# A hybrid mLSTM / RWKV-7 layer on one core: triangular joins, finished pairs and chunk operands move to other banks, buffers and places in the order

## The chip, the core and the metric

The kernel runs on one core of a Trainium2 chip. A core has five engines that execute their instructions each in its own order: PE (TensorE, matmuls), DVE (VectorE), ACT (ScalarE), POOL (GpSimd) and SP (SyncE, which here only starts DMA transfers). They wait for each other by semaphores. SBUF holds the working data, PSUM the results of matmuls, in eight banks. The metric is the device time of one execution in microseconds: the kernel before takes 3405.07 us, the median of three runs (3402.93 to 3407.92).

## The reference

One layer over 512 latent tokens (x) and 256 context tokens (ctx) of width 2048, in float32. Both go through one input projection, whose output feeds two groups of heads: an mLSTM with four heads and an RWKV-7 with sixteen heads of width 64, each in both directions. The RWKV state is a 64 x 64 matrix per head and direction:

```
def step(s, xs):
    r_t, w_t, k_t, v_t, kk_t, a_t = xs
    s = (s * w_t[:, :, None, :]
         - jnp.einsum("bhvk,bhk->bhv", s, kk_t)[..., None] * (kk_t * a_t)[:, :, None, :]
         + v_t[..., :, None] * k_t[..., None, :])
    return s, jnp.einsum("bhvk,bhk->bhv", s, r_t)
...
y_f, s_f = rwkv7_scan(..., state[2], False)
y_b, s_b = rwkv7_scan(..., state[3], True)
y = y_f + y_b
...
hc = modulate(rms_norm(ctx, g_norm1[layer]), csh1, csc1)
yc, ctx_state = hybrid_mixers(hc, p, zero_state(ctx.shape[0]))
hx = modulate(rms_norm(x, g_norm1[layer]), sh1, sc1)
yx, _ = hybrid_mixers(hx, p, ctx_state)
x = x + gt1 * (yx @ w_out[layer])
hx = modulate(rms_norm(x, g_norm2[layer]), sh2, sc2)
x = x + gt2 * conv_ffn(hx, rows, GRID_W, p)
...
return rms_norm(x, g_final)
```

The scans over x start from the states that the context leaves. The summed y of a head is normalised, gets a bonus term and a gate, and enters the output projection beside the mLSTM heads.

## The kernel before

**Stages.** First the adaLN vectors and the context's projections; then the projections of x, beside which the RWKV heads are worked; then the mLSTM heads and the output projection; then the FFN (from about 1900 us to the end). Float32 products are made of three matmuls with split operands (high and low parts: `whi`, `wlo`, `H`), so a weight tile that a DMA brings is split by ACT (L299) and DVE (L300).

**The RWKV part.** Two heads make a pair (eight pairs), a pair and a direction make a unit. Tokens are cut into chunks of 64 (eight for x, four for ctx). A pair goes through five steps:
- *Preparation*: `pair_shared` (L661) and `prep` (L681) make the decayed keys and, with matmuls into banks "pre" (L747), the 64 x 64 products within a chunk. All that a chunk needs is stored in DRAM (`Sx_d`, `Sc_d`).
- *Solve*: `tsolve` loads the two 32 x 32 diagonal triangles of every 64 x 64 block of two pairs (four context units of pairs), inverts them in thirty row steps on DVE (L798, L799) and stores them.
- *Join*: the off-diagonal block follows from the two inverses by 32 x 32 matmuls (L816, then L821, 64 each for a pair of x), in two R banks. It loads a pair's block into `t_Y`, which has one buffer, transposes it on DVE (L810), copies the first product on ACT (L818) and the second on DVE (L823), and stores the result.
- *Chain*: `chain` steps through the chunks of two pairs at once, four units in a step, both R banks in each step (`chain_step`: matmuls L856 and L859, copies on ACT L870 and L878, state update on DVE L890, outputs L900 and L902). The operands of two chunks come with one load, `chain_load`, into `r_GK` (six buffers of two chunks, L830).
- *Finalization*: `finalize_pair` loads y, normalises it on DVE and ACT, transposes it by four matmuls (L977) in a bank "pre" and multiplies in the gate (L978). `mid()` in a chain runs it a step further: before the yield, then behind it.

**What sets the order.** A queue holds jobs: `solve_q` after preparation, `chain_q` after the solve. Before the preparation of pair p, `x_job(p)` calls a solve (p even) or a chain (p odd) of the two pairs that are ready. Behind the loop over pairs stand `do_solve(2)` (pairs 6 and 7) and, with the mLSTM projections, `do_chain(2)`. The scheduler of the language (it simulates a timeline of its own) then fixes the order of each engine, so what is written earlier has precedence but need not come first. All weight, chunk and adaLN loads are started by SP, one after the other. PSUM has two banks "acc" (projections), four "pre" and two "R". The adaLN accumulation of the later chunks (`ada_late`, rows L232 on DVE: `adacc<-am`) is spread among these jobs. The first half of the output projection (L1268 to L1270) needs mLSTM heads 0 and 1 and pairs 0 to 3, the second half the rest.

Of the kernel before, what the change touches and what calls it, by code (L numbers as in the profile page):

```python
# [15 lines left out]
P = 128  # L16
# [80 lines left out]
def body(tc, A, dbg=None):  # L97
# [679 lines left out]
    def tsolve(pairs):  # L777

        nc_ = 2 * pairs[0][0].nch
        n = 4 * nc_ * len(pairs)  # L780
        x = rp("t_X", [P, 32, 32], 1)[0:n]

        def blocks():
            q = 0
            for us in pairs:
                for r in range(0, P, 32):
                    o = us[0].kc + r % 64
                    yield x[q:q + nc_], us[0].S_d[r:r + 32, :, o:o + 32].rearrange("s c t -> c s t")
                    q += nc_

        for t, g in blocks():
            sp.dma_start(t, g)
        T1 = rp("t_T", [P, 256], 1)[0:n]
        dve.memset(x.rearrange("p s t -> p (s t)")[:, 0:1024:33], 1.0)
        for t in range(30, 0, -1):
            m = 31 - t
            w = T1[:, 0:t * m].rearrange("p (s t) -> p s t", t=m)
            dve.tensor_tensor(w, x[:, 0:t, t:t + 1].to_broadcast([n, t, m]), x[:, t:t + 1, t + 1:32].to_broadcast([n, t, m]), ALU.mult)  # L798
            dve.tensor_tensor(x[:, 0:t, t + 1:32], x[:, 0:t, t + 1:32], w, ALU.add)  # L799
        for t, g in blocks():  # L800
            sp.dma_start(g, t)

        XT = rp("t_X", [P, 2, 16, 32], 1)
        for k, us in enumerate(pairs):
            kc = us[0].kc
            T_d = us[0].S_d[:, :, kc:kc + 64]
            T = rp("t_Y", [P, 16, 64], 1)[:, 0:nc_]
            sp.dma_start(T, T_d)
            W = XT[:, k, 0:nc_]
            dve.transpose(W, T[:, :, 0:32])  # L810
            ws = [PS("R", [P, 16, 32])[:, 0:nc_] for _ in range(2)]
            a_, b_ = ([slice(64 * h + o, 64 * h + o + 32) for h in range(2)] for o in (0, 32))
# [12 lines left out]

    def chain_load(u, tt):

        cu = u.c0 + 2 * tt
        o = rk("r_GK", [P, 2, 512], 6)[:, :, 0:3 * u.kc + 128]
        sp.dma_start(o, u.S_d[:, cu:cu + 2, :])  # L830
        return o

    def chain_v(p, seg, nch):
# [70 lines left out]
    def chain(pairs, mid):  # L904

        x = pairs[0][0].seg == "x"
        nch = pairs[0][0].nch
        Vs, ys = [], []
        for us in pairs:
            Vs.append(chain_v(us[0].p, us[0].seg, nch))  # L910
            ys.append(rk("r_yt", [P, 8, 64], 2) if x else None)
            for u in us:
                if not x:
                    Mst[(u.p, u.d)] = rk("r_M", [P, 64], 16)
                    pool.memset(Mst[(u.p, u.d)], 0.0)
                u.M = Mst[(u.p, u.d)]
        n = nch // 2
        for i in range(n):
            if x and i == 1:
                mid()  # L920
            ops = [[chain_load(u, i if u.d == 0 else n - 1 - i) for u in us] for us in pairs]
            for c in range(2 * i, 2 * i + 2):
                units = []
                for k, (us, os_, V, y) in enumerate(zip(pairs, ops, Vs, ys)):
                    us[0].y = y
                    for j, (u, o) in enumerate(zip(us, os_)):
                        cu = nch - 1 - c if j else c
                        units.append((u, o[:, cu % 2], cu, V, 2 * k + (j if 2 * c < nch - 1 else 1 - j)))
                chain_step(units, c < nch // 2, x and c == nch - 1)
        if x:  # L930
            for us, y in zip(pairs, ys):
                y_d = us[0].y_d = DT("yr_d", [4, P, 128], 8)
                for h in range(2):
                    sp.dma_start(y_d[:, :, 64 * h:64 * h + 64].rearrange("a (b t) v -> t (a b) v", t=64), y[LOHI[1 - h]])
            mid()

    def bonus(p, uf, ub, s):
        kd = uf.kd
# [11 lines left out]
    def finalize_pair(p, uf, ub, bo):  # L950
# [21 lines left out]
        gs = sq.rearrange("p a b -> p (a b)")  # L972
        sp.dma_start(gs, g_d[p])
        yield
        pt = PS("pre", [P, 512])
        for tt in range(4):
            pe.transpose(pt[:, 128 * tt:128 * tt + 128], y[:, tt, :], ident)  # L977
        dve.scalar_tensor_tensor(gs, pt, V("gnb", p), gs, ALU.add, ALU.mult)  # L978
# [37 lines left out]
    def ctx_part(H, k0, k1, part):  # L1016
        for n, (tag, (kind, *ts)) in enumerate(ctx_plan):
            if k0 == 0:
                if tag == "r_y":
                    d = rk("r_y", [P, 512], 2)  # L1020
                else:
                    if n % 2 == 0:
                        pair = am() if tag == "am" else rk("r_GK", [P, 2, 512], 6)
                    d = pair[:, n % 2]
                part.append(d)
            d = part[n][:, 0:512 if kind == "tm" else NC_ * len(ts)]
            pt = PS("acc", [P, 512])[:, 0:d.shape[-1]]
# [86 lines left out]
    Hx = HT(NX)  # L1114
    modulated(xload2, rx, gsc[:, :, 0], mod[:, 0:16], Hx, range(8))

    solve_q, chain_q = [], []

    fin_q = []

# [15 lines left out]
        while fin_q or fin[0] is not None:  # L1136
            fin_step()

    def do_chain(n=1):
        if len(chain_q) >= n:  # L1140
            job = [t for _ in range(n) for t in chain_q.pop(0)]
            chain([us for _, us, _ in job], fin_step)
            fin_q.extend(t for t in job if t[2] is not None)

    def do_solve(n=1):
        if len(solve_q) >= n:
            jobs = [solve_q.pop(0) for _ in range(n)]
            tsolve([us for job in jobs for _, us, _ in job])
            chain_q.extend(jobs)

    def ctx_job(p):
        do_chain()
        job = []
        for pp in range(p, p + 2):
            s = pair_shared(pp, "c")
            job.append((pp, prep(pp, s, "c", DT("Sc_d", [P, 8, 320], 8)), None))
        do_solve()
        solve_q.append(job)

    def x_job(p):  # L1160
        if p < 2:
            do_chain()
        elif p % 2 == 0:
            do_solve(2)
        else:
            do_chain(2)
        s = pair_shared(p, "x")
        S_d = DT("Sx_d", [P, 16, 512], 8)
        us = prep(p, s, "x", S_d, 0) + prep(p, s, "x", S_d, 1)
        job = [(p, us, bonus(p, us[0], us[1], s))]  # L1170
        if p == 0:
            do_solve()
        solve_q.append(job)


    for i, _ in enumerate(ctx_finish(Hc, part)):
# [51 lines left out]
    for p in range(NPAIR):  # L1228
# [12 lines left out]
        for h in range(MH):  # L1241
            if HEAD_AT[h] == p and p < 7:
                x_head(h)
    do_solve(2)
    for h in range(MH):
        if h == CHAIN_H:
            do_chain(2)
        if HEAD_AT[h] == 7:
            x_head(h)
        for _ in range(LATE_H[h]):  # L1250
# [37 lines left out]
    assert not chain_q and not solve_q  # L1288
    ahead_[0] = AHEAD
    Hm.more(2)  # L1290
    for k in KORD[8:]:
# [215 lines left out]
```

## Time and profile before

| | |
|---|---|
| median of three runs | 3405.07 us |
| profiled execution, and its span | 3401.15 us, 3399.3 us |
| busy in the span: PE, DVE, ACT | 3083.4, 2170.8, 1181.5 us |
| matmuls | 21030 |
| granted PE clock, mean of the execution | 0.933 |
| loads of weights for the adaLN, count and size | 128, 512 KB each |
| loads of x chunks, count and size | 64, 512 KB each |

The profile is of one execution. Its span runs from the first to the last instruction. Each digit of the slices is the busy share of a fortieth of the span (85 us) in tenths. A wait is put down to what came last by the semaphores. The granted clock is a share of TensorE's full speed.

### The profile page before, as it was taken

What the parts mean: (1) busy time and instruction counts of PE and PEld (TensorE: products, weight loads), DVE (VectorE), ACT (ScalarE), POOL (GpSimd) and SP (SyncE); (2) the same over time, 40 slices, a digit from 0 to 9 for tenths busy, and PEclk for the clock granted to TensorE, in tenths of its full rate; (3) what the DMA queues carried; (4) which work ended last, traced back from release to release, by engine and by line L of the source; (5) the groups of instructions that cost most, each with busy time, mean ns of one, the idle gap of its engine ahead of it and who ended that gap; (6) DMA issues with size and microseconds to landing.
All of it is one profiled execution on the core that took longest, in us unless ns stands there. A gap on an engine that the chain in (4) does not pass through costs nothing.

```text
span 3399.3 us, 54225 instructions
## 1 busy us (share of the span) xinstructions
PE 3083.4 (91%) x21030; PEld 2509.1 (74%) x21030; DVE 2170.8 (64%) x4178; ACT 1181.5 (35%) x2235; POOL 45.7 (1%) x113
## 2 busy tenths in 40 slices
PE   8998889999999886576498899999999999999998
PEld 5687777777788774555376688888888888888887
DVE  2577886898764796655554678455555555655657
ACT  4355654344323433133222433222222222322323
POOL 0000000010000000000000000000000000000000
PEclk9999889999999896567798999999999999999999
DMA  8877556677764766667644255222232232223222
GB/s 286 303 238 221 161 161 183 184 227 214 236 197 152 229 215 192 191 193 235 226 141 156 81 190 197 92 97 96 97 96 97 94 99 93 99 93 99 93 99 100
DMA packets 394385, 548.51 MB, mean 161 GB/s; under 512 B 151664, under 2 KB 272776, under 8 KB 393872
## 3 DMA queue, kind: packets, MB, share of 16 engines
q1 hardware_dynamic: 384480, 531.67, 49.2%
q10 hardware_dynamic: 9648, 13.37, 1.1%
q8 instruction: 166, 2.72, 0.3%
q14 instruction: 91, 0.75, 0.1%
HBM read 457.49 MB, written 87.47 MB: 160 GB/s over the span
## 4 chain that ended last, share of the span: by engine, by line
PE 57%; DVE 10%; DMA 9%; issue 2%; ACT 2%; SPq 1%; DVEq 0%; ACTq 0%
PE acc L372 10%; PE acc L370 10%; PE acc L371 10%; PE acc L1382 5%; PE acc L1384 4%; PE acc L1383 4%; DMA am<-in_wmod 3%; PE acc L1268 1%; PE acc L1269 1%; PE acc L1270 1%; DVE adacc L232 1%; DVE r_Gp L750 1%; PE R L859 1%; PE pre L621 1%; DVE r_M L890 1%
## 5 line engine op out<-in xcount | busy, mean ns | idle before, releaser
L299 ACT CAST whi<-wraw 128x512 fp32r<-128x512 f32 (+1 forms) x948 | 569.5, 604 | 1350.4 <-PE acc L371 719.6
L300 DVE TENSOR_TENSOR wlo<-wraw,whi 128x512 fp32r<-128x512 f32 (+1 forms) x948 | 627.9, 666 | 463.9 <-ACT whi L299 446.8
L372 PE MATMUL acc<-H,wlo 128*128 128x512 f32 x1920 | 760.0, 396 | 5.3 <-DVE wlo L300 5.3
L370 PE MATMUL acc<-H,whi 128*128 128x512 f32 x1920 | 758.5, 395 | 1.5 <-ACT upad L1323 0.5
L371 PE MATMUL acc<-H,whi 128*128 128x512 f32 x1920 | 756.9, 394 | 0.0
L372 PEld LDWEIGHTS acc<-H,wlo 128*128 128x128 f32 x1920 | 364.0, 190 | 85.1 <-DVE wlo L300 7.1
L370 PEld LDWEIGHTS acc<-H,whi 128*128 128x128 f32 x1920 | 364.3, 190 | 80.8 <-issue 2.5
L371 PEld LDWEIGHTS acc<-H,whi 128*128 128x128 f32 x1920 | 363.9, 190 | 77.3 <-issue 1.4
L1386 DVE SCALAR_TENSOR_TENSOR x<-acc,mod,x 128x512 f32<-128x512 f32 (+1 forms) x192 | 135.6, 706 | 221.8 <-PE acc L1384 221.7
L1330 DVE SCALAR_TENSOR_TENSOR f_cv<-upad,fvec,f_cv 128x512 f32<-128x512 f32 x352 | 263.8, 749 | 7.2
L1382 PE MATMUL acc<-fh,whi 128*128 128x512 f32 x640 | 253.2, 396 | 0.0
L1383 PE MATMUL acc<-fl,whi 128*128 128x512 f32 x640 | 253.1, 396 | 0.0
L1384 PE MATMUL acc<-fh,wlo 128*128 128x512 f32 x640 | 253.1, 396 | 0.0
L232 DVE SCALAR_TENSOR_TENSOR adacc<-am,csil,adacc 128x512 f32<-128x512 f32 x240 | 179.4, 747 | 92.2 <-DMA am<-in_wmod 90.5
L404 PE MATMUL acc<-whi,H 128*128 128x256 f32 x512 | 151.8, 297 | 0.0
L405 PE MATMUL acc<-wlo,H 128*128 128x256 f32 x512 | 148.9, 293 | 3.1 <-DVE wlo L300 3.1
L403 PE MATMUL acc<-whi,H 128*128 128x256 f32 x512 | 150.5, 294 | 0.5 <-DVE ev L434 0.5
L1384 PEld LDWEIGHTS acc<-fh,wlo 128*128 128x128 f32 x640 | 120.2, 188 | 29.1
L1382 PEld LDWEIGHTS acc<-fh,whi 128*128 128x128 f32 x640 | 120.2, 188 | 29.0
L1383 PEld LDWEIGHTS acc<-fl,whi 128*128 128x128 f32 x640 | 120.2, 188 | 29.0
L750 DVE TENSOR_TENSOR r_Gp<-pre,c_gmask 64x512 f32<-64x512 f32 (+1 forms) x192 | 115.2, 600 | 34.8 <-DMA Sx_d<-r_Gp 21.3
L1268 PE MATMUL acc<-H,whi 128*128 128x512 f32 x256 | 104.3, 410 | 20.9 <-ACT H L299 16.0
(348 smaller groups left out, 4639.8 us busy)
## 6 DMA issues: line engine op xcount, KB each, us to landing
am<-in_wmod SPq DMA_DIRECT2D x128, 512.0 KB
wraw<-in_wup SPq DMA_DIRECT2D x88, 512.0 KB
wraw<-in_wgate SPq DMA_DIRECT2D x88, 512.0 KB
wraw<-in_wdn SPq DMA_DIRECT2D x88, 512.0 KB
wraw<-in_wcm SPq DMA_DIRECT2D x72, 512.0 KB
r_GK<-Sx_d SPq DMA_DIRECT2D x64, 512.0 KB
wraw<-in_wtm SPq DMA_DIRECT2D x56, 512.0 KB
Sx_d<-r_Gp SPq DMA_DIRECT2D x32, 512.0 KB
```

The costliest lines, as they stand in the source:

```text
L232: dve.scalar_tensor_tensor(acc, wm[:, k % 2], csil[:, k:k + 1], acc, ALU.mult, ALU.add)
L299: act.copy(hi, t)
L300: dve.tensor_tensor(lo, t, hi.bitcast(F32), ALU.subtract)
L370: pe.matmul(pt[:, :n], hi(k8), H.h(k), start=k == 0, stop=False)
L371: pe.matmul(pt[:, :n], hi(k8), H.l(k), start=False, stop=False)
L372: pe.matmul(pt[:, :n], lo(k8), H.h(k), start=False, stop=k == KT - 1)
L403: pe.matmul(o, H.h(k)[:, xs], hi(k4), start=first, stop=False, skip_group_check=True)
L404: pe.matmul(o, H.l(k)[:, xs], hi(k4), start=False, stop=False, skip_group_check=True)
L1330: dve.scalar_tensor_tensor(cv, u[:, a:a + GH, b:b + GW], fvec[:, f, tap:tap + 1], cv, ALU.mult, ALU.add)
L1382: pe.matmul(pt, hi(m)[:, k, :], th[:, cs], start=k == 0, stop=False)
L1383: pe.matmul(pt, hi(m)[:, k, :], tl[:, cs], start=False, stop=False)
L1384: pe.matmul(pt, lo(m)[:, k, :], th[:, cs], start=False, stop=k == GF - 1)
```

## The change

Four things are done. The join leaves `tsolve` and becomes `tjoin`, in two banks "pre" (L814) instead of "R"; it is called by `do_join`, after the next preparation and before the chain, and the solve of a job follows the chain. A finished pair's transposes take a bank "R" (L973). The chunk operands are loaded chunk by chunk: 12 buffers of one chunk instead of six of two, 128 loads for x and 64 for ctx instead of 64 and 32. `mid()` is called before steps 2 and 6 of an x chain instead of before step 2 and behind the last one. The three queues `made`, `solved`, `joined` replace two; the chains of the context's pairs run one job earlier.

```
+    def tjoin(pairs):
+        nc_ = 2 * pairs[0][0].nch
         XT = rp("t_X", [P, 2, 16, 32], 1)
         for k, us in enumerate(pairs):
...
-            ws = [PS("R", [P, 16, 32])[:, 0:nc_] for _ in range(2)]
+            ws = [PS("pre", [P, 16, 32])[:, 0:nc_] for _ in range(2)]
...
-    def chain_load(u, tt):
-        cu = u.c0 + 2 * tt
-        o = rk("r_GK", [P, 2, 512], 6)[:, :, 0:3 * u.kc + 128]
-        sp.dma_start(o, u.S_d[:, cu:cu + 2, :])
+    def chain_load(u, cu):
+        o = rk("r_GK", [P, 512], 12)[:, 0:3 * u.kc + 128]
+        sp.dma_start(o, u.S_d[:, u.c0 + cu, :])
...
-        n = nch // 2
-        for i in range(n):
-            if x and i == 1:
+        for c in range(nch):
+            if x and c in (2, 6):
                 mid()
...
-            mid()
...
-        pt = PS("pre", [P, 512])
+        pt = PS("R", [P, 512])
         for tt in range(4):
             pe.transpose(pt[:, 128 * tt:128 * tt + 128], y[:, tt, :], ident)
...
     def x_job(p):
-        if p < 2:
-            do_chain()
-        elif p % 2 == 0:
-            do_solve(2)
-        else:
-            do_chain(2)
         s = pair_shared(p, "x")
         S_d = DT("Sx_d", [P, 16, 512], 8)
         us = prep(p, s, "x", S_d, 0) + prep(p, s, "x", S_d, 1)
-        job = [(p, us, bonus(p, us[0], us[1], s))]
-        if p == 0:
+        made.append((p, us, bonus(p, us[0], us[1], s)))
+        do_join()
+        do_chain()
+        if p % 2:
             do_solve()
-        solve_q.append(job)
...
-    do_solve(2)
+    do_join()
     for h in range(MH):
         if h == CHAIN_H:
-            do_chain(2)
+            do_chain()
```

Lines behind `tsolve` shift by two to three: L814, L859, L977, L1268 of before are L817, L861, L975, L1266 after. The order of three places shows what moves. In a row stand the line, the operation, its output and its inputs with buffer numbers, and the shape.

PE, before, the end of the last chain (pairs 6 and 7). R is the chain's bank, r_GK a chunk's operands, r_y a finished pair's y, r_kr and r_KR operands of an mLSTM head:

```order
L859 MATMUL R_14292<-r_U_14326,r_GK_14199 64x64
L859 MATMUL R_14292<-r_U_14326,r_GK_14201 64x64
L859 MATMUL R_14292<-r_U_14326,r_GK_14203 64x64
L859 MATMUL R_14292<-r_U_14326,r_GK_14205 64x64
L977 MATMUL pre_17403<-c_ident_90,r_y_17377 128x128 x4
L977 MATMUL pre_17436<-c_ident_90,r_y_17410 128x128 x4
L605 MATMUL pre_17482<-r_kr_17174,r_KR_17176 128x512
L605 MATMUL pre_17486<-r_kr_17174,r_KR_17176 128x512
L605 MATMUL pre_17490<-r_kr_17174,r_KR_17176 128x512
L605 MATMUL pre_17494<-r_kr_17174,r_KR_17176 128x512
```

PE, after, the same place. L238 sums an adaLN chunk; H, whi and wlo are operands of the output projection:

```order
L861 MATMUL R_14523<-r_U_14557,r_GK_14520 64x64
L238 MATMUL pre_17296<-c_ones_80,adacc_16488 128x1 x4
L975 MATMUL R_17568<-c_ident_90,r_y_14396 128x128 x4
L605 MATMUL pre_17680<-r_kr_17372,r_KR_17374 128x512
L605 MATMUL pre_17684<-r_kr_17372,r_KR_17374 128x512
L605 MATMUL pre_17688<-r_kr_17372,r_KR_17374 128x512
L1266 MATMUL acc_17732<-H_17338,whi_17739 128x512
L1267 MATMUL acc_17732<-H_17339,whi_17739 128x512
L1268 MATMUL acc_17732<-H_17338,wlo_17740 128x512
L1266 MATMUL acc_17732<-H_17338,whi_17739 128x512
L1267 MATMUL acc_17732<-H_17339,whi_17739 128x512
L1268 MATMUL acc_17732<-H_17338,wlo_17740 128x512
```

The two pairs' transposes stood directly behind the last step. Now one stands there, of an earlier pair, and two later ones (of pairs 6 and 7) follow 88 and 114 rows further on, behind head and projection matmuls.

PE, before, the end of the joins of pairs 4 and 5 (t_Y holds the blocks) and the start of pair 7's preparation (L669, L701) and of the chain of pairs 4 and 5 (L856):

```order
L821 MATMUL R_12087<-t_Y_12084,t_X_12009 32x32
L821 MATMUL R_12088<-t_Y_12084,t_X_12009 32x32
L821 MATMUL R_12087<-t_Y_12084,t_X_12009 32x32
L821 MATMUL R_12088<-t_Y_12084,t_X_12009 32x32
L977 MATMUL pre_13127<-c_ident_90,r_y_12591 128x128 x4
L669 MATMUL pre_13166<-r_t_2208_13164,c_bones_92 128x512
L701 MATMUL pre_13176<-r_lw_6228,r_up_13173 128x512
L701 MATMUL pre_13177<-r_la_6230,r_up_13173 128x512
L856 MATMUL R_12416<-r_V_12400,r_GK_12408 64x64 x2
```

PE, after, the second join of pairs 4 and 5:

```order
L861 MATMUL R_12511<-r_V_12495,r_GK_12505 64x64
L861 MATMUL R_12512<-r_V_12495,r_GK_12505 64x64
L861 MATMUL R_12511<-r_V_12495,r_GK_12505 64x64
L861 MATMUL R_12512<-r_V_12495,r_GK_12505 64x64
L238 MATMUL pre_13287<-c_ones_80,adacc_11255 128x1 x4
L669 MATMUL pre_13332<-r_t_2294_13330,c_bones_92 128x512
L824 MATMUL pre_12424<-t_Y_12421,t_X_12346 32x32 x5
L824 MATMUL pre_12425<-t_Y_12421,t_X_12346 32x32 x5
...
L824 MATMUL pre_12424<-t_Y_12421,t_X_12346 32x32
L824 MATMUL pre_12425<-t_Y_12421,t_X_12346 32x32
L701 MATMUL pre_13342<-r_lw_6615,r_up_13339 128x512
L701 MATMUL pre_13343<-r_la_6617,r_up_13339 128x512
L861 MATMUL R_12511<-r_V_12499,r_GK_12507 64x64
```

The chain stood behind the last matmul of the joins. Now its first steps (L861), an adaLN sum and the first matmul of pair 7's preparation stand between the two runs of the second join.

DVE, before, in pair 7's preparation (r_BK, r_kd, r_cum: decayed keys and their sums; r_Gp: products within a chunk; r_y: a finished pair):

```order
L733 SCALAR_TENSOR_TENSOR r_BK_13189<-r_t_2222_13195,r_sg_13178 128x8x64
L727 SCALAR_TENSOR_TENSOR r_kd_13198<-r_kd_13198,c_vecs_88,r_kr_13160 128x512
L961 TENSOR_REDUCE r_mu_13137<-r_y_13135 128x8
L736 TENSOR_TENSOR r_BK_13189<-r_kd_13198,r_sg_13178 128x8x64
L266 TENSOR_SCALAR srvr_13145<-r_mu_13137,bconst_100 128x8
L756 TENSOR_TENSOR r_cum_13238<-r_BK_13189,r_gC_13190 128x512
...
L964 TENSOR_TENSOR r_y_13134<-r_y_13134,r_rs_13143 128x512
L967 TENSOR_TENSOR r_y_13134<-r_y_13134,r_gw_13153 128x512
L970 TENSOR_TENSOR r_y_13135<-r_y_13135,r_bo_9746 128x512
L971 TENSOR_TENSOR r_y_13134<-r_y_13134,r_y_13135 128x512
L750 TENSOR_TENSOR r_Gp_13206<-pre_13207,c_gmask_94 64x4x128 x2
L750 TENSOR_TENSOR r_Gp_13206<-pre_13208,c_gmask_94 64x4x128 x2
```

DVE, after, the same place:

```order
L733 SCALAR_TENSOR_TENSOR r_BK_13355<-r_t_2308_13361,r_sg_13344 128x8x64
L727 SCALAR_TENSOR_TENSOR r_kd_13364<-r_kd_13364,c_vecs_88,r_kr_13326 128x512
L232 SCALAR_TENSOR_TENSOR adacc_13293<-am_13302,csil_110,adacc_13293 128x512
L736 TENSOR_TENSOR r_BK_13355<-r_kd_13364,r_sg_13344 128x8x64
L232 SCALAR_TENSOR_TENSOR adacc_13293<-am_13302,csil_110,adacc_13293 128x512
L756 TENSOR_TENSOR r_cum_13404<-r_BK_13355,r_gC_13356 128x512
L750 TENSOR_TENSOR r_Gp_13372<-pre_13373,c_gmask_94 64x4x128 x2
L750 TENSOR_TENSOR r_Gp_13372<-pre_13374,c_gmask_94 64x4x128 x2
L232 SCALAR_TENSOR_TENSOR adacc_13293<-am_13306,csil_110,adacc_13293 128x512 x2
L750 TENSOR_TENSOR r_Gp_13388<-pre_13389,c_gmask_94 64x4x128 x2
L750 TENSOR_TENSOR r_Gp_13388<-pre_13390,c_gmask_94 64x4x128 x2
L232 SCALAR_TENSOR_TENSOR adacc_13293<-am_13310,csil_110,adacc_13293 128x512
```

The finished pair's rows have left this piece, and adaLN rows (adacc) have come in. From the first row of pair 7's preparation (L672) to the transpose that opens the joins of pairs 6 and 7 (L810, after L813) there are 29 rows L232 after and 15 before; two finished pairs are worked there after, one before.

## Rows read from the trace of the kernel before

**Rows 1.** The page, parts 1 and 2: busy times, tenths in 40 slices.

```profile
PE 3083.4 (91%) x21030; PEld 2509.1 (74%) x21030; DVE 2170.8 (64%) x4178; ACT 1181.5 (35%) x2235; POOL 45.7 (1%) x113
...
PE   8998889999999886576498899999999999999998
...
DVE  2577886898764796655554678455555555655657
...
PEclk9999889999999896567798999999999999999999
```

**Rows 2.** Times by stretch: start:end, length, then busy times, granted clock, DMA share, GB/s.

```profile
250.00:1296.00 1046.00, 949.70 (x9069) 789.49 (x9068) 795.95 (x1750) 454.30 (x901) 39.92 (x69) 0.94 0.65 199
1296.00:1326.00 30.00, 15.83 (x268) 11.97 (x266) 15.87 (x32) 8.57 (x14) 0.00 (x0) 0.60 0.76 210
1326.00:1448.00 122.00, 70.72 (x1096) 59.96 (x1096) 84.44 (x224) 31.59 (x75) 0.94 (x5) 0.54 0.59 179
1448.00:1483.00 35.00, 24.33 (x302) 17.85 (x302) 21.61 (x46) 9.71 (x15) 0.00 (x0) 0.60 0.55 158
1483.00:1657.00 174.00, 125.92 (x1327) 98.49 (x1327) 98.68 (x251) 61.86 (x158) 1.79 (x8) 0.77 0.75 244
1657.00:1697.00 40.00, 2.88 (x16) 2.20 (x15) 23.43 (x45) 7.23 (x10) 0.00 (x0) 0.54 0.56 170
```

**Rows 3.** Chain of waits, joins of pairs 4 and 5: start, length, what.

```profile
1298.05 1.98 PE R L816 x63
...
1304.29 4.96 DMA Sx_d<-t_Y
1309.32 4.52 DMA t_Y<-Sx_d
...
1320.34 1.06 PE pre L977 x4
```

**Rows 4.** Chain of waits, joins of pairs 6 and 7.

```profile
1436.34 4.52 DMA t_Y<-Sx_d
...
1448.33 3.20 PE R L816 x61
1451.68 3.05 PE R L821 x61
...
1455.55 0.70 DVE r_mu L957
...
1461.51 0.69 DVE r_y L964
...
1469.08 0.76 DVE r_y L978
```

**Rows 5.** Timeline of PE, the second join of pairs 6 and 7.

```profile
1470.35 1.92 PE L816 MATMUL R<-t_X,t_Y 32*32 32x32 f32 x64
1472.19 5.46 PE L605 MATMUL pre<-r_kr,r_KR 128*128 128x512 f32 x8
1477.59 1.47 PE L821 MATMUL R<-t_Y,t_X 32*32 32x32 f32 x64
```

**Rows 6.** Waits of PE, 1300 to 1450: us in total, times, longest.

```profile
PE R L859 <- DMA r_GK<-Sx_d: 8.9, 7, 3.9
```

**Rows 7.** Line 830, the loads of chunks: ns min/median/max, first and last.

```profile
L830 SPq DMA_DIRECT2D r_GK<-Sx_d x64: 319/422/2339, 925.3 to 1622.2; - x64
...
L830 SPq DMA_DIRECT2D r_GK<-Sc_d x32: 377/462/1083, 426.8 to 850.3; - x32
```

**Rows 8.** Waits of SP, 550 to 1300.

```profile
SPq L349 <- DVE wlo L300: 144.0, 44, 9.5
```

**Rows 9.** Groups of VectorE, 1326 to 1448: count, busy, mean ns, idle before.

```profile
L890 DVE SCALAR_TENSOR_TENSOR r_M<-r_M,r_gC,R 64x64 f32<-64x64 f32 x56 | 12.2, 279 | 0.3
L232 DVE SCALAR_TENSOR_TENSOR adacc<-am,csil,adacc 128x512 f32<-128x512 f32 x15 | 11.2, 747 | 5.1 <-DMA am<-in_wmod 5.0
...
L902 DVE TENSOR_TENSOR r_yt<-R,r_yt 64x128 f32<-64x128 f32 x14 | 3.4, 285 | 4.4 <-PE R L859 4.3
```

**Rows 10.** Timeline of PE behind the last chain step, idle time in brackets.

```profile
1656.70 0.68 PE L859 MATMUL R<-r_U,r_GK 64*64 64x64 f32 x10
1679.60 1.11 PE L977 MATMUL pre<-c_ident,r_y 128*128 128x128 f32 x4 [22.22 <-DVE r_y L971]
1695.60 1.12 PE L977 MATMUL pre<-c_ident,r_y 128*128 128x128 f32 x4 [14.90 <-DVE r_y L971]
```

**Rows 11.** Groups of PE, 1657 to 1797.

```profile
L1268 PE MATMUL acc<-H,whi 128*128 128x512 f32 x72 | 28.3, 393 | 1.4 <-ACT H L626 1.4
L1270 PE MATMUL acc<-H,wlo 128*128 128x512 f32 x72 | 28.1, 391 | 0.0
L1269 PE MATMUL acc<-H,whi 128*128 128x512 f32 x72 | 28.0, 389 | 0.0
```

More of the change, by code (lines that the diff above doesn't have):

```diff
@@ L916, in chain @@
                 u.M = Mst[(u.p, u.d)]
-        n = nch // 2
-        for i in range(n):
-            if x and i == 1:
+        for c in range(nch):
+            if x and c in (2, 6):
                 mid()
[L921 to L929, printed above, removed]
+            units = []
+            for k, (us, V, y) in enumerate(zip(pairs, Vs, ys)):
+                us[0].y = y
+                for j, u in enumerate(us):
+                    cu = nch - 1 - c if j else c
+                    units.append((u, chain_load(u, cu), cu, V, 2 * k + (j if 2 * c < nch - 1 else 1 - j)))
+            chain_step(units, c < nch // 2, x and c == nch - 1)
         if x:
@@ L1018, in ctx_part @@
             if k0 == 0:
-                if tag == "r_y":
-                    d = rk("r_y", [P, 512], 2)
-                else:
-                    if n % 2 == 0:
-                        pair = am() if tag == "am" else rk("r_GK", [P, 2, 512], 6)
-                    d = pair[:, n % 2]
+                if tag == "am":
+                    if n % 2 == 0:
+                        pair = am()
+                    d = pair[:, n % 2]
+                else:
+                    d = rk(tag, [P, 512], 2 if tag == "r_y" else 12)
                 part.append(d)
@@ L1115, in body @@
     modulated(xload2, rx, gsc[:, :, 0], mod[:, 0:16], Hx, range(8))
-    solve_q, chain_q = [], []
+    made, solved, joined = [], [], []
     fin_q = []
@@ L1137, in do_finalize, with do_chain, do_join, do_solve @@
             fin_step()
-    def do_chain(n=1):
-        if len(chain_q) >= n:
-            job = [t for _ in range(n) for t in chain_q.pop(0)]
+    def do_chain():
+        if joined:
+            job = joined.pop(0)
             chain([us for _, us, _ in job], fin_step)
             fin_q.extend(t for t in job if t[2] is not None)
[L1145 to L1149, printed above, removed]
+    def do_join():
+        if solved:
+            job = solved.pop(0)
+            tjoin([us for _, us, _ in job])
+            joined.append(job)
+    def do_solve():
+        job = list(made)
+        made.clear()
+        tsolve([us for _, us, _ in job])
+        solved.append(job)
     def ctx_job(p):
-        do_chain()
-        job = []
         for pp in range(p, p + 2):
             s = pair_shared(pp, "c")
-            job.append((pp, prep(pp, s, "c", DT("Sc_d", [P, 8, 320], 8)), None))
+            made.append((pp, prep(pp, s, "c", DT("Sc_d", [P, 8, 320], 8)), None))
+        do_join()
+        do_chain()
         do_solve()
-        solve_q.append(job)
     def x_job(p):
-        if p < 2:
-            do_chain()
-        elif p % 2 == 0:
-            do_solve(2)
-        else:
-            do_chain(2)
         s = pair_shared(p, "x")
@@ L1169, in x_job @@
         us = prep(p, s, "x", S_d, 0) + prep(p, s, "x", S_d, 1)
-        job = [(p, us, bonus(p, us[0], us[1], s))]
-        if p == 0:
+        made.append((p, us, bonus(p, us[0], us[1], s)))
+        do_join()
+        do_chain()
+        if p % 2:
             do_solve()
-        solve_q.append(job)
     for i, _ in enumerate(ctx_finish(Hc, part)):
@@ L1243, in body @@
                 x_head(h)
-    do_solve(2)
+    do_join()
     for h in range(MH):
         if h == CHAIN_H:
-            do_chain(2)
+            do_chain()
         if HEAD_AT[h] == 7:
@@ L1287, in body @@
     run([mlstm_head(h, EARLY_AT[h] == 4 and h < NEARLY) for h in range(MH) if EARLY_AT[h] == 4 or h >= NEARLY] + [out_first()])
-    assert not chain_q and not solve_q
+    assert not made and not solved and not joined
     ahead_[0] = AHEAD
```

## The prediction

> **What bounds the kernel now.** I read the busy table first [rows 1]: TensorE is busy 91% of the span, VectorE 64%, so most of the time is TensorE's projections and FFN, which the change does not touch. The slices of the same page show where TensorE is not full: digits of 8 and 9 at first, then a hole in slices 15 to 19, counted from 0 (6, 5, 7, 6, 4), where the granted clock falls as well (6, 5, 6, 7, 7). The times by stretch [rows 2] put borders on it. From 250 to 1296 us the projections stand beside the preparations and chains and TensorE is busy 949.7 of 1046 us at a clock of 0.94. At 1296 the projections are used up. From there to 1697 us TensorE has 15.8 + 70.7 + 24.3 + 125.9 + 2.9 = 240 us of work in 401, at a clock of 0.54 to 0.77, that is near the lower of its levels for half the time. After 1697 it is full again. I call 1296 to 1697 the tail; what the change gives or costs is read there.
>
> In the tail the R banks set the pace. A chain step takes both, a join takes both, so chains and joins follow each other: joins of pairs 4 and 5 (1298 to 1320), their chain (1326 to 1448), joins of 6 and 7 (1448 to 1483), their chain (1483 to 1657), and then two finished pairs. The chain of waits shows what sits between the two joins of a job [rows 3]: two runs of matmuls, a copy, and then 4.96 + 4.52 us of DMA, since t_Y has one buffer and must be stored before it is loaded for the next pair.
>
> **The change, part by part.** The sums are made against the profiled execution, 3401.15 us (span 3399.3); the median of the runs is 3405.07, 3.9 more.
>
> (a) Joins of pairs 4 and 5. Now the last projection ends at about 1296 and the second join at 1320.3 + 0.3, 24.6 us later, with everything of the round trip [rows 3] bare. In the new order the first join's second run of matmuls still has projection matmuls right ahead of it, and the second join is split by the first matmuls of pair 7's preparation and by the chain, which no longer needs the joins' banks. The first run (1.98), its copy and a part of the second run are then covered. I take 19 us instead of 24.6: −5, between −10 (the store and load of t_Y covered by the last projections) and 0.
>
> (b) Joins of pairs 6 and 7. First join's matmuls end at 1454.7, the second's at 1479.1, and between them stand 24 us [rows 4, 5], of which the t_Y trip itself is about 9.5 by [rows 3]. The rest is VectorE and TensorE on other things: the finalization of a pair runs on VectorE in the gap, from the reduce at 1455.55 to the multiply at 1469.08, and 5.46 us of L605 stand between the two matmul runs of pair 7. In the new order these rows have moved out to before and behind the joins (VectorE rows in this stretch sum to about 5 us instead of 26). About 10 of the 24 us remain necessary, about 4 are lost again to waits of the same kind: −10, between −14 and 0.
>
> (c) Operands by chunk. In the stretch of chain 4,5 a matmul waited 8.9 us for r_GK in seven places [rows 6]. A load of one chunk has half the bytes, and its buffer comes free a chunk earlier. But chain 4,5 must not only end, pair 6's T must also have come back: its load lands at 1440.9 (1436.34 + 4.52) [rows 4], and the join starts at 1448.3, so at most 7.4 us count. I take half of the 8.9, about −5 (−7.4 to 0). Price: 64 + 32 loads become 192, 96 more issues on SP at 0.42 to 0.46 us [rows 7], 42 us of SP. I cost them at nothing, because SP waits for others: 144 us in the stretch 550 to 1300 for weight tiles that VectorE has yet to split [rows 8].
>
> The Trainium skill, "DMA: Bandwidth & Descriptors", section "Bandwidth", speaks against this part: it says to batch transfers to 1 MiB or more, since smaller ones reach less of the peak. No row here times a 256 KB load; the one row that bears on it is that a matmul waited 8.9 us for loads of 512 KB [rows 6]. By the rule alone this term would be no gain, and the sum −33.
>
> (d) VectorE on the path of pair 7. Its preparation, the solve and the load of T must be done before the last joins. In the new order 14 more rows of the ada accumulation stand in that stretch (29 against 15) and one more finished pair's finalization. At 0.747 us for a row of the ada accumulation [rows 9] that is 10.5 us; the finalization adds some ten rows of 0.6 to 0.76 (L964 to L978 [rows 4]), 7 us; small ones (r_M, r_yt, at 0.28 [rows 9]) and two copies make up the rest of 22.7 us. VectorE was busy 84.4 of 122 us [rows 2], idle 37.6, so by the idle time it fits, but it executes in the written order, and an ada row waits for its own load: 5.0 us for 15 rows [rows 9], so up to 9 us for 29. Lower end 0 (all fits in the idle time), upper end 22.7 + 9 = 32. I take +12: the idle time stands in pieces of 1 to 6 us, behind DMAs on that very path, so about half of the added rows fall into it.
>
> (e) The end of the last chain. Now the transposes of pairs 6 and 7 stand at the head of TensorE's queue after the chain, and behind them 51 us of out projection and head work that is ready. TensorE waits 22.22 + 14.90 = 37.1 us for VectorE's r_y [rows 10]. In the new order one pair's transposes stand there, whose finalization started earlier; right behind them come three rows of L605 and the out projection, and pairs 6 and 7 follow some 90 and 115 rows after the chain. That is also what moving these transposes to the R banks allows: they no longer take a bank that L605 and L621 rotate through. The work that can fill the hole is larger than the hole: the out projection of the first half alone has 28.3 + 28.1 + 28.0 us between 1657 and 1797 [rows 11]. −30, between −37 and 0; 7 stay for the first finalization and for the clock, granted at 0.54 in this stretch [rows 2], which has to rise first.
>
> (f) The projections, 250 to 1296. Chains of the context pairs run a job earlier and the preparations of pairs 2 and 3 later. The work is the same in both orders; what differs is how it is spread. By stage VectorE's rows sum to about 800 us and TensorE's to 950 [rows 2], so a stretch in which VectorE is the larger loses time and one where TensorE is the larger doesn't; cutting it in several ways I get −26 to +23 for the difference. I take 0 (−20 to +25). The joins that stand in this part give nothing back: with projections beside them TensorE was full.
>
> Smaller things at nothing: a transposing pair holds one R bank for 1.06 us of matmul [rows 3] plus a VectorE read of 0.76, at four places in the tail where the chain could want it, hidden as long as the chain waits for VectorE anyway.
>
> The sum: −5 −10 −5 +12 −30 + 0 = −38, so 3401.15 − 38 = 3363 for a profiled execution; plus 3.9 gives a median of about 3367.
>
> **The rivals.**
>
> 1. The projections get better balanced as well (f at −17): 3350. For it: VectorE is nearly full in slices 7 to 9 (8, 9, 8) and has room in 10 to 12 (7, 6, 4) [rows 1], where the later preparations would now stand. Against it: the weights' splits are on VectorE throughout, and they come with the projections.
>
> 2. It comes out level. f at +25 with d at +20 leaves −5 −10 −5 +20 −30 +25 = −5: 3400. For it: in the new order chain 0,1 lies beside the preparations of pairs 3 and 4, where VectorE serves both. Against it: TensorE has 96 us of idle time in 1046 to absorb it.
>
> 3. Slower: VectorE's written order in the tail becomes the bound. Its added rows cost d = +32, and the finalizations of pairs 6 and 7, which now share VectorE with 51.7 us of rows (21.4 before) between the end of the chain and pair 7's last multiply, delay the out projection's second half by what e gives, so e = 0. The other terms stay at −20 together: +12, 3417. It decides from the point at which d and e together pass +27: with d at its upper end that is as soon as less than 5 us of the hole behind the chain are filled. Against it: the second out half cannot start before the first half and head 3, which fill TensorE to 1797 now, and that leaves pair 7's transposes 100 us.
>
> 4. The small loads. If SP were what the chain waits for, the 42 us of issues would stand on the path and take everything given elsewhere: 3401 − 38 + 42 + 3.9 = 3409, and with loads that come no sooner (c = 0) 3414. For it: waits for r_GK are there already [rows 6]. The rule of the Trainium skill's page "DMA: Bandwidth & Descriptors", section "Bandwidth", points the same way. Against it: the 144 us that SP waits, and that the waits for r_GK in chain 4,5 are a fourteenth of its length.
>
> **How the numbers follow.** The forecast 0.50 (3367, own range 3340 to 3397 by the bounds of a to e); rival 1 0.16; rival 2 0.12; rival 3 0.15; rival 4 0.07. What a measurement of this kernel can tell from no change is about 0.2%, 6.8 us. Faster by more: 0.50 + 0.16 = 0.66; level 0.12; slower 0.15 + 0.07 = 0.22. The range: down to 3330 (rival 1 with e at −37 and d at 0), up to 3420, which takes in the price of rivals 3 and 4; what is left out is a worse mix of these.
>
> **What would show it.** In the changed kernel's trace: (a, b) the interval from the first join's last matmul to the second's under 15 us for pairs 6 and 7, with no finalization between; (c) waits of a chain's matmul on r_GK under 4 us in chain 4,5, and SP still waiting for VectorE's splits more than for anything else; (d) from the start of chain 4,5 to the joins of pairs 6 and 7 about 134 us instead of 122; (e) no wait of a transpose for r_y over 8 us behind the last chain, and projection matmuls within a few us of its end; (f) the last projection at 1276 to 1321 us. The prediction is wrong if the projections end outside of that, if VectorE is busy over 90% between chain 4,5 and the joins of 6 and 7, or if the second out half waits for pair 7.

## The result and the profile after

The changed kernel takes 3429.12 us (median of four runs, 3425.37 to 3431.41) against 3404.0 of the kernel before in the same series: ratio 1.0074, 95% interval 1.0057 to 1.0092. Slower by 25 us (0.7%), where 38 us faster was forecast. The profiled execution has a span of 3427.1 us.

The stretches of the changed kernel between its own landmarks (last projection, start of the chain of pairs 4 and 5, joins of 6 and 7, start and end of their chain, second half of the output projection), columns as in [rows 2]:

```profile
250.00:1316.00 1066.00, 953.75 (x9128) 796.23 (x9127) 788.42 (x1741) 453.18 (x903) 54.28 (x69) 0.94 0.64 193
1316.00:1348.00 32.00, 13.86 (x228) 9.33 (x231) 14.65 (x25) 8.78 (x12) 0.42 (x2) 0.61 0.55 152
1348.00:1488.00 140.00, 70.25 (x1084) 60.73 (x1084) 90.68 (x242) 33.00 (x76) 0.40 (x3) 0.55 0.63 189
1488.00:1528.00 40.00, 27.47 (x332) 20.67 (x335) 14.87 (x30) 4.66 (x12) 0.00 (x0) 0.63 0.48 132
1528.00:1692.00 164.00, 112.38 (x1238) 88.94 (x1238) 95.30 (x252) 63.99 (x156) 1.85 (x8) 0.73 0.70 227
1692.00:1845.00 153.00, 123.61 (x514) 96.06 (x513) 82.18 (x172) 37.53 (x84) 0.00 (x0) 0.92 0.61 201
```

Before, the last stretch went from 1657 to 1816:

```profile
1657.00:1816.00 159.00, 108.06 (x455) 83.44 (x453) 75.34 (x157) 35.23 (x79) 0.00 (x0) 0.84 0.50 161
```

Set beside [rows 2], the lengths changed by +20, +2, +18, +5, −10 and −6 us, +29 in all at the second half of the output projection; from there to the end both need the same (1583 and 1582 us). The start of a chain is not the same landmark in both: before, 1326 and 1483 are its first matmuls; after, these stand between the joins (1329 and 1505), and 1348 and 1528 are where it runs on. So the stretches are best read in three parts: the projections +20, from their end to the joins of pairs 6 and 7 +20, from there to the second half −11.

TensorE's busy time to that point is 1295 us before (the six stretches summed) and 1301 after: nearly the same. What grew is its idle time, length less busy: 271 us before, 294 after; in the three parts by +16, +22 and −16. The sum is given for all runs below. It does not rank them alone: changed_own_bank has less of it than the kernel before and is slower, with a busy time of 1329 us.

The two long waits behind the last chain [rows 10: 22.22 and 14.90] are gone as forecast. In the waits of TensorE from 1692 to 1845 the transposes, L975, have 2.3 us; others have come in, and the idle time of this stretch fell from 51 to 29 us:

```profile
PE acc L1266 <- ACT H L299: 10.2, 1, 10.2
PE acc L621 <- ACT H L626: 9.6, 2, 7.3
PE acc L1266 <- ACT m_dn L622: 3.1, 1, 3.1
PE R L975 <- DVE r_y L969: 2.3, 2, 1.5
```

But the work that fills it came out of the chain just ahead. Groups of PE within the last chain, before (1483 to 1657) and after (1528 to 1692); this is one of three equal rows of the output projection:

```profile
L1268 PE MATMUL acc<-H,whi 128*128 128x512 f32 x48 | 21.0, 442 | 7.1 <-ACT H L299 6.6 <-DVE ev L1277 0.5
```

```profile
L1266 PE MATMUL acc<-H,whi 128*128 128x512 f32 x29 | 13.8, 490 | 2.5 <-ACT H L299 2.5
```

Nineteen matmuls of three kinds, 57 in all, stood within the chain before and stand behind it now. From the joins of pairs 6 and 7 to the second half, with this chain in it, the time fell by 11 us.

And the start of pair 7's preparation, the place to look at. First before, then after: the timeline of PE.

```profile
1317.22 3.11 PE L821 MATMUL R<-t_Y,t_X 32*32 32x32 f32 x64 [0.63 <-ACT t_X L818]
1320.27 1.11 PE L977 MATMUL pre<-c_ident,r_y 128*128 128x128 f32 x4
1321.17 1.92 PE L669 MATMUL pre<-r_t,c_bones 128*128 128x512 f32 x2
```

```profile
1329.24 1.92 PE L819 MATMUL pre<-t_X,t_Y 32*32 32x32 f32 x64
1331.08 0.49 PE L861 MATMUL R<-r_V,r_GK 64*64 64x64 f32 x8
1331.51 1.86 PE L238 MATMUL pre<-c_ones,adacc 128*128 128x1 f32 x8
1333.23 2.05 PE L669 MATMUL pre<-r_t,c_bones 128*128 128x512 f32 x2
```

L669 is the first matmul of the preparation. Before, it comes right behind a finished pair's transposes in the same pool, "pre"; after, behind the first matmuls of the second join (L819) and an adaLN sum, both in "pre". None of them makes its data: its operand r_t was ready 83 us earlier before and 79 us earlier after (timeline of ACT, two lines before, one after):

```profile
1236.78 0.72 ACT L665 ACTIVATE r_kk<-r_kr,c_vecs 128x512 f32<-128x512 f32 x1 [4.03 <-DMA r_kr<-kr_x]
1237.53 0.63 ACT L667 ACTIVATE r_t<-r_kk 128x512 f32<-128x512 f32 x1
```

```profile
1253.14 0.63 ACT L667 ACTIVATE r_t<-r_kk 128x512 f32<-128x512 f32 x1
```

Both starts come behind the last projection (1296 and 1316), so the preparation, the solve and the ada rows that stand among them have only the chain beside them.

### The profile page after: what moved, and what is told of

Its sections match the earlier page's. It is cut to its first block, busy times and chain, and to the rows that moved or that the text cites. A ratio compares the mean times of both kernels' runs of the same rounds, so it can differ in the third digit from the quotient of the medians.

```text
span 3427.1 us, 54321 instructions
## 1 busy us (share of the span) xinstructions
PE 3087.9 (90%) x21030; PEld 2518.5 (73%) x21030; DVE 2163.3 (63%) x4178; ACT 1181.3 (34%) x2235; POOL 60.0 (2%) x113
## 4 chain that ended last, share of the span: by engine, by line
PE 47%; DMA 8%; DVE 7%; ACT 1%; issue 1%; SPq 1%; DVEq 0%; ACTq 0%
PE acc L370 9%; PE acc L372 9%; PE acc L371 9%; PE acc L1380 4%; PE acc L1382 4%; PE acc L1381 4%; DMA am<-in_wmod 3%; DVE adacc L232 1%; PE acc L1266 1%; PE acc L1267 1%; PE acc L1268 1%; DMA x_d<-ev 1%; DMA r_GK<-Sx_d 1%; DVE r_M L892 1%; DVE r_Gp L750 0%
## 5 line engine op out<-in xcount | busy, mean ns | idle before, releaser
L232 DVE SCALAR_TENSOR_TENSOR adacc<-am,csil,adacc 128x512 f32<-128x512 f32 x240 | 179.2, 747 | 101.4 <-DMA am<-in_wmod 99.9
L750 DVE TENSOR_TENSOR r_Gp<-pre,c_gmask 64x512 f32<-64x512 f32 (+1 forms) x192 | 115.1, 599 | 37.1 <-PE pre L747 11.7
L1266 PE MATMUL acc<-H,whi 128*128 128x512 f32 x256 | 106.9, 421 | 18.9 <-ACT H L299 13.2
```

What stands on the lines that cost most here:

```text
L232: dve.scalar_tensor_tensor(acc, wm[:, k % 2], csil[:, k:k + 1], acc, ALU.mult, ALU.add)
```

## The experiments

In the table, "T" is the pool of the finished pairs' transposes, "J" that of the joins, "p7" the start of pair 7's preparation on VectorE (L672) in us, "idle" TensorE's idle time from 250 us to the second half of the output projection (length less busy time, as above). Ratios are to the kernel before in the same series, with their 95% intervals; its medians in the six series are 3399 to 3404 us, so medians of different series compare to about 5 us.

| kernel | T | J | p7 | idle | median | ratio |
|---|---|---|---|---|---|---|
| before | pre | R | 1326 | 271 | 3404 | |
| changed | R | pre | 1337 | 294 | 3429.1 | 1.0074 (1.0057 to 1.0092) |
| order_only | pre | R | 1326 | 295 | 3426.2 | 1.0078 (1.0060 to 1.0096) |
| undo_join_bank | R | R | 1079 | 247 | 3370.8 | 0.9911 (0.9891 to 0.9931) |
| undo_transpose_bank | pre | pre | 1349 | 310 | 3437.6 | 1.0104 (1.0077 to 1.0130) |
| undo_loads | R | pre | 1331 | 273 | 3404.5 | 1.0009 (0.9996 to 1.0022) |
| old_mid | R | pre | 1324 | 276 | 3409.1 | 1.0038 (1.0026 to 1.0049) |
| changed_own_bank | own | pre | 1355 | 253 | 3415.0 | 1.0029 (1.0018 to 1.0040) |
| one_transpose_bank | R | R | 1066 | 241 | 3355.3 | 0.9861 (0.9838 to 0.9884) |
| one_join_bank | pre | pre | 1433 | 366 | 3512.5 | 1.0324 (1.0305 to 1.0342) |
| one_load | pre | R | 1324 | 280 | 3399.9 | 0.9992 (0.9979 to 1.0006) |
| transpose_bank_one_load | R | R | 1062 | 224 | 3351.6 | 0.9847 (0.9831 to 0.9863) |
| own_bank | own | R | 1106 | 203 | 3339.2 | 0.9820 (0.9806 to 0.9835) |
| order_and_transpose_bank | R | R | 1042 | 247 | 3375.5 | 0.9928 (0.9905 to 0.9951) |
| late_join | R | pre | 1205 | 212 | 3337.2 | 0.9817 (0.9794 to 0.9840) |
| late_join_two_loads | R | pre | 1205 | 214 | 3340.0 | 0.9806 (0.9784 to 0.9827) |
| late_join_R | R | R | 1072 | 229 | 3355.7 | 0.9857 (0.9842 to 0.9873) |
| late_join_transposes_pre | pre | pre | 1226 | 261 | 3386.3 | 0.9961 (0.9948 to 0.9975) |
| late_join_own_bank | own | pre | 1278 | 236 | 3394.8 | 0.9972 (0.9958 to 0.9987) |

**First: which part costs?** One part undone in the changed kernel, and the sequence of jobs alone.

```
order_only            banks, loads and mid() of before in the changed kernel
undo_join_bank        -ws = [PS("pre", ...   +ws = [PS("R", ...
undo_transpose_bank   -pt = PS("R", ...      +pt = PS("pre", ...   (finalize_pair)
undo_loads            chain_load of before, six buffers of two chunks
```

> The new sequence of jobs alone: join split from the solve, called after the next preparation and before the chain; banks of joins (R) and of finished pairs' transposes (pre), loads of two chunks and the two steps of the finalization as in the kernel before. Theory A (the sequence costs: x chains now lie beside preparations, and VectorE's written order holds up both): as slow as the changed kernel, 3420 to 3435 us, last projection later than 1310 us. Theory B (the banks cost: transposes in R hold up chain steps, joins in pre hold up preparations): 3400 to 3410. Theory C (small loads cost): 3400 to 3410.

> The changed kernel with the joins' products back in the R banks, all else as changed. Theory A: within 8 us of the changed kernel's 3429 or slower, since a join that waits behind the preparation must now also wait for the chain. Theory B: 10 us or more faster, 3405 to 3419, if the joins in pre are what holds up the preparations. Theory C: 3429.

> The changed kernel with the finished pairs' transposes back in a bank pre. Theory A: 3422 to 3436. Theory B: 3405 to 3419, since waits of these transposes for a chain's outputs (5.8 and 4.3 us in the chain of pairs 4 and 5) go. Theory C: 3429.

> The changed kernel with the chunk operands loaded two chunks at a time again (6 buffers), all else as changed. Theory A: 3422 to 3436. Theory B: the same. Theory C (96 more issues and small loads cost): 3404 to 3415, and waits of chain matmuls on the loads fall from 37 us in the three x chains after 900 us to under 20.

None of the three theories holds. The sequence alone is slow (A), though its projections end at 1283 and not later than 1310; one word for the joins' pool gives 58 us, more than twice what B allowed and past the kernel before; undo_transpose_bank is no faster, against B; the old loads give 25 (C), but the waits for them fall only from 37 to 30 us, not under 20. The column p7 shows what the fast one has: pair 7's preparation stands at 1079, beside projections. This led to theory R: the tiles of a PSUM pool are handed out in the order of the program, so a preparation's tiles in pre stand behind whatever the program puts into pre ahead of them. Before, these are transposes that wait for a chain (pair 2's, whose y is loaded at 1303, behind the chain of pairs 2 and 3); in the changed kernel, joins that wait for a solve. Only with both out of pre is the preparation free. No trace shows the handing out itself; what the runs can show is where L669 and L672 come to stand.

order_only also shows where the new sequence loses without any change of banks or loads. Its p7 is that of the kernel before, 1326, but from there to the joins of pairs 6 and 7 it takes 142 us instead of 122, and VectorE executes 29 adaLN rows (L232) in between instead of 15 [rows 9]. Groups of VectorE, 1326.5 to 1467:

```profile
L232 DVE SCALAR_TENSOR_TENSOR adacc<-am,csil,adacc 128x512 f32<-128x512 f32 x29 | 21.6, 746 | 6.0 <-DMA am<-in_wmod 5.8
```

The other kernels with this sequence and a late preparation (changed, undo_transpose_bank, undo_loads, old_mid, changed_own_bank) take 136 to 152 us there with 27 to 29 such rows, one_load with the old sequence 125 us with 15. No run moves these rows alone, so that they are the cause is not shown.

**Second: theory R.** Single parts on the kernel before; and the changed kernel with joins and chains called behind the odd preparations only, so that pair 7's stands ahead of the joins of 4 and 5.

```
one_transpose_bank        before;  -pt = PS("pre", ...  +pt = PS("R", ...
one_join_bank             before;  -ws = [PS("R", ...   +ws = [PS("pre", ...
late_join                 changed, in x_job:
     -        do_join()
     -        do_chain()
              if p % 2:
     +            do_join()
     +            do_chain()
                  do_solve()
order_and_transpose_bank  order_only with transposes in R
```

> The kernel before with one part of the change alone: the finished pairs' transposes take a bank R instead of pre. Theory R (rotation: tiles of a PSUM pool come free in the order of the program, so a preparation's banks wait for whatever stands before them in pool pre; before, that is a finished pair's transposes, which wait for a chain, and in the changed kernel it is the joins): pair 7's preparation no longer waits for the chain of pairs 2 and 3, it starts before the projections end, and the kernel takes 3360 to 3385 us. Theory A (the sequence of jobs, chains beside preparations, is what moves the time): 3395 to 3410, as before.

> The kernel before with the joins' products in banks pre, nothing else changed. Theory R: joins and transposes both stand ahead of preparations in pool pre, so nothing is freed and one tie is added: 3405 to 3440 us, pair 7's preparation starts behind the joins of pairs 4 and 5, as in the kernel before. Theory A: 3395 to 3410.

> The changed kernel with the banks as changed, but joins and chains called in the odd pairs' jobs only, after their preparation, so that pair 7's preparation stands ahead of the joins of pairs 4 and 5 in the program and in pool pre. Theory R: 3365 to 3395 us, pair 7's preparation starts before the last projection. Theory A (banks don't matter, chains still lie beside preparations): 3420 to 3435.

> The new sequence of jobs and the transposes in R; joins in R, loads of two chunks and the two steps of the finalization as in the kernel before. Theory R: the tie that made the sequence alone take 3426 us (transposes in pre) is gone: 3360 to 3385 us, like the changed kernel with its joins back in R (3371). Theory A: 3420 to 3435, as the sequence alone.

All four go the way that R says, in p7 and in time, but only order_and_transpose_bank lies in its range: two gain more (3355 and 3337 against at least 3360 and 3365), and one_join_bank loses 112 us, where R allowed up to 40. There two preparations are held: pair 6's starts at 1348 instead of 1181, beside the joins of pairs 4 and 5, and pair 7's at 1433, behind the transposes again. One word in one line of the kernel before gives 1.4%; one word in another costs 3.2%. PE of one_join_bank, where the tie is worst:

```profile
1425.28 1.12 PE L977 MATMUL pre<-c_ident,r_y 128*128 128x128 f32 x4 [1.63 <-DVE r_y L971]
1426.18 1.92 PE L669 MATMUL pre<-r_t,c_bones 128*128 128x512 f32 x2
```

**Third: the loads, and joins in R under the new place.**

> The kernel late_join (3337 us) with the chunk operands loaded two chunks at a time again. Theory L (loads by chunk cost some 25 us, as the changed kernel against the one with the old loads said: 3429 against 3404): 3305 to 3320. Theory S (that difference belongs to the order that the scheduler then wrote, not to the loads): 3322 to 3352, and waits of chain matmuls for the operands rise from 0.3 us after 900 us to more than 5.

> The kernel before with the transposes in R (3355 us) and loads by chunk. Theory L: 3373 to 3390. Theory S: 3335 to 3372, waits of chain matmuls for the operands under the 21.4 us of the same kernel with loads of two chunks.

> The kernel before with loads by chunk alone. Theory L: 3418 to 3435. Theory S: 3388 to 3415. Theory R is not touched: pair 7's preparation stays at about 1326 us.

> late_join with the joins' products in R: every tile that waits for a chain or a solve is out of pool pre. Theory R: pair 7's preparation starts before the 1205 us of late_join, at 1030 to 1090 as in the other kernels with joins and transposes in R. For the time two things pull: preparations free (faster), joins that wait for the chain's banks (slower): 3330 to 3375.

Theory L falls: with loads by chunk and by two chunks three pairs of kernels take 3337 and 3340, 3352 and 3355, 3400 and 3404 us, and no ratio differs beyond its interval (0.9817 and 0.9806, 0.9847 and 0.9861, 0.9992). The waits go as S says: 12.9 us in late_join_two_loads instead of 0.3, 10.9 in transpose_bank_one_load instead of 21.4. late_join_R has its preparation earlier than late_join (1072 against 1205) and is still 18 us slower (0.9857 against 0.9817): its joins of pairs 4 and 5 begin at 1359 us, behind the chain that holds R, in late_join at 1280 beside it. So joins in pre seem worth something, once this preparation does not stand behind them.

**Fourth: the pool or the bank R? And the rest of the 25 us.**

```
own_bank            before;  PB = {"acc": 2, "pre": 3, "R": 2, "F": 1},  pt = PS("F", ...
old_mid             changed; -if x and c in (2, 6):  +if x and c == 2:  and mid() behind the last step
changed_own_bank, late_join_own_bank: the pool F in these
late_join_transposes_pre: late_join with  pt = PS("pre", ...
```

> The kernel before with the finished pairs' transposes in one bank of their own; pool pre has three banks instead of four, R is as before. Theory R (rotation): pair 7's preparation starts before 1150 us, although pre is smaller, and the kernel takes 3345 to 3380 us. Rival (the bank R itself is what helps, by the time at which transposes run there): 3395 to 3420.

> late_join (3337 us) with the finished pairs' transposes in pre. Theory R: pair 7's preparation now stands behind a transpose of the chain of pairs 2 and 3 (its step 6), so it starts at 1250 us or later instead of 1205, and the kernel takes 3375 to 3425. If the joins were the only tie: 3330 to 3350.

> The changed kernel with the finalization's steps before step 2 and behind the last step of a chain, as before. If the 25 us that the old loads gave belong to the order of the rows and not to a part: anywhere from 3400 to 3435, with pair 7's preparation at about 1337 us still. If the new places of the steps cost: 3400 to 3412.

> The changed kernel with the finished pairs' transposes in one bank of their own (pre 3, R 2). Theory H (transposes between chain steps in R hold up the chain): 3400 to 3415, no wait of these transposes for a chain's outputs. Rival (the tie of pair 7's preparation to the joins is all, and pre is one bank smaller): 3425 to 3445. Pair 7's preparation stays behind the joins of pairs 4 and 5, after 1310 us, in both.

> late_join (3337 us) with the finished pairs' transposes in one bank of their own (pre 3, R 2). Theory H: 3315 to 3332. Rival (joins and preparations now share three banks, which costs more): 3340 to 3370.

own_bank settles it: R is untouched and pre is smaller, and p7 moves to 1106; the time, 3339, is 6 us below R's range and 56 below the rival's. Its timeline of PE at pair 7's start, among projections, and its tail from the last projection on:

```profile
1097.02 0.35 PE L859 MATMUL R<-r_Rs,r_GK 64*64 64x64 f32 x6
1097.30 1.12 PE L669 MATMUL pre<-r_t,c_bones 128*128 128x512 f32 x2
1097.86 0.79 PE L372 MATMUL acc<-H,wlo 128*128 128x512 f32 x1
```

```profile
1340.00:1360.00 20.00, 6.14 (x132) 5.50 (x132) 11.19 (x22) 6.44 (x9) 0.00 (x0) 0.59 0.75 227
1360.00:1445.00 85.00, 52.62 (x1004) 47.05 (x1005) 46.00 (x162) 12.75 (x35) 0.00 (x0) 0.50 0.46 126
1445.00:1487.00 42.00, 28.34 (x404) 24.54 (x403) 20.14 (x45) 9.53 (x29) 0.00 (x0) 0.62 0.69 195
1487.00:1625.00 138.00, 106.79 (x1143) 78.27 (x1142) 84.89 (x232) 46.71 (x131) 1.78 (x8) 0.78 0.66 214
1625.00:1753.00 128.00, 110.74 (x497) 91.48 (x495) 63.86 (x132) 28.83 (x78) 0.00 (x0) 0.96 0.66 213
```

From the end of the joins of pairs 4 and 5 to those of 6 and 7 it takes 85 us (1360 to 1445), where it took 128 before (1320 to 1448) and 151 in the changed kernel (1337 to 1488): no preparation is left there, VectorE is busy 46.0 us. The projections end 44 us later than before, since the preparation now shares their time. late_join_transposes_pre gives back 49 of late_join's gain as R says, though p7 moves less than expected (1226, not 1250).

Theory H is not shown: changed_own_bank gets 14 us back, at the edge of its range, but late_join_own_bank loses 58, outside of both ranges; its joins and preparations share three banks (p7 1278), which fits the rival's reason, not its size. old_mid gets back 20, undo_loads 25, changed_own_bank 14, with p7 still behind the last projection (1324, 1331 and 1355); each writes a new order of all rows, and no wait of one part explains them. Whose these 14 to 25 us are stays open. The kernel before has a tie as well, so the tie does not explain why the changed kernel is 25 us slower than it: that much may be the order of the rows alone, which is not shown.

## Why the prediction was wrong, step by step

In the three parts of the result the forecast had 0 for the projections (f), +2 from there to the joins of pairs 6 and 7 (a, c, d), and −40 from there to the second half (b, e). They came out at +20, +20 and −11.

**The step that failed: the joins went into "pre" at no price.** In (a) I counted it as a gain that the joins of pairs 4 and 5 leave the R banks and mix with the first matmuls of pair 7's preparation. No term asked what that preparation then waits for. It starts at 1337, behind these joins; with the joins alone back in R it starts at 1079, and the kernel takes 3371 instead of 3429 us. So this costs 58 us, and the forecast missed by 62.

I took the start of the preparation, 1326, as given, and priced what was added behind it. The row that held the answer stands in [rows 3] as its last line: transposes in pre, and L669 of pair 7 begins 0.9 us behind them. I used that row only as the price of a held bank, and it was a tie: pair 7's operand had been there since 1238.

**(e), −30, was too large.** The place was right, the wait went from 37.1 to 2.3 us. But I counted a filled hole as time won without asking where the filling stood before: 57 matmuls of it within the chain just ahead. With (b) I had −40 and got −11.

**(d), +12, was too small.** With (a) and (c) I had +2 for this part, it took +20. From 1348 to 1488 VectorE was busy 90.7 of 140 us, and did wait for ada loads. Groups of VectorE, 1348 to 1488:

```profile
L232 DVE SCALAR_TENSOR_TENSOR adacc<-am,csil,adacc 128x512 f32<-128x512 f32 x26 | 19.4, 746 | 9.5 <-DMA am<-in_wmod 9.4
```

The mechanism may well be right: order_only has the same rows there and is also 20 us longer in this place.

**(f), 0 in −20 to +25,** came out at +20, near its upper end; why is open, since order_only ends its projections at 1283. The end of the projections is no measure by itself: own_bank ends them at 1340 and is 60 us faster than before (3339.2 against 3399.1 in its series), with pair 7's preparation done beside them. In the changed kernel nothing came earlier for it.

**(a), −5,** came out at −3 by its own measure: the second join ends 21 us behind the last projection instead of 24. **(b), −10:** from the first join's end to the second's it takes 19 us instead of 24 for pairs 6 and 7, so −5.

**(c), −5,** was wrong in sign here. Waits of TensorE in the changed kernel, 1300 to 1692, each long one at a chain's start:

```profile
PE R L858 <- DMA r_GK<-Sx_d: 21.9, 2, 11.0
...
PE R L861 <- DMA r_GK<-Sx_d: 7.5, 2, 7.1
```

There the load waits for the join's store (chain of waits):

```profile
1319.27 4.07 DMA Sx_d<-t_Y
...
1324.04 4.64 DMA r_GK<-Sx_d
...
1328.82 0.49 PE R L858 x8
```

The small loads themselves show no cost: one_load 0.9992 (0.9979 to 1.0006). SP still waited most for VectorE's splits, 92.3 us from 550 to 1300 (144.0 before). The Trainium skill, "DMA: Bandwidth & Descriptors", section "Bandwidth", says to batch transfers to 1 MiB or more. In one_load, where a chunk load has 256 KB instead of 512 KB, no difference shows.

Rival 3 (VectorE's order in the tail, 3417) had the sign and was 12 us short, but by luck: it had d at +32 and e at 0 with the projections unchanged, and VectorE was busy for 65% of the stretch. Its reason, added rows, fits what order_only shows. None of my signs of being wrong came: the projections end at 1316, VectorE stays under 90%, and the second half waits for no finished pair. They watched the terms that I had priced. My own range, 3340 to 3397, does not follow from the bounds of (a) to (e): added up they give 3337 to 3437, and 3429 lies within.

The forecast's number, 3367, is near what the changed kernel gives with its joins in R (3371). That is luck too: there the projections end at 1359, 63 us later than before, and the time is won behind them, with the preparation already done. own_bank, which has none of the priced terms, wins more.

## What to carry to other kernels

Before pricing a change of banks, list for each pool what the program hands out in it, in order, and ask of each stage which foreign stage it stands behind; two stages with different waits in one rotating pool are tied. Where a stage starts right behind an instruction that does not feed it, look for such a tie first. Of a hole to be filled, ask from where; judge by the sum of the bounding engine's idle time, and look at its busy time beside it.

## What was not expected of the hardware

One bank fewer for the preparations cost nothing that could be seen beside the tie (own_bank, 3339 with three banks of pre). Where the preparation and the joins share those three, it shows: late_join_own_bank against late_join, 3395 against 3337 us, with TensorE's busy time to the second half of the output projection at 1328 us instead of 1288 and the mean granted clock there at 0.87 instead of 0.89.
